# The last four weights of a transformer layer: loaded together into buffers of their own, and one part of a gate vector computed a step earlier

## Chip, cores, metric
One core of one Trainium2 chip runs the whole layer as one program. The metric is the time of an execution in device microseconds, as the median of several executions. Everything is fp32; the large matrix products run as pairs of rounded values (below).

## What is computed
The reference is one layer of a diffusion backbone over 512 latent tokens and 256 context tokens of width 1024: attention and gated linear attention side by side, merged and added to the stream, then a gated MLP with a 3x3 depthwise convolution. The change touches the end of the merge and the end of the MLP:

```python
mod = jax.nn.silu(c) @ w_ada[layer] + b_ada[layer]
sh1, sc1, gt1, sh2, sc2, gt2 = jnp.split(mod[:, None, :], 6, axis=-1)
...
out_lat = merge_branches(...)            # ends in  (...) @ w_out
x_lat = x_lat + gt1 * mix
h = modulate(rms_norm(x_lat, norm2_g[layer]), sh2, sc2)
val, gate = jnp.split(h @ w_up, 2, axis=-1)
gate = depthwise_conv_grid(gate, conv_w, conv_b, rows, cols)
x_lat = x_lat + gt2 * ((jax.nn.gelu(gate, approximate=False) * val) @ w_down)
return rms_norm(x_lat, final_g)
```

`gt2` is a vector of 1024 numbers, the last sixth of `mod`. `w_down` has 2816 rows, that is 22 blocks of 128 rows.

## The kernel before, in words
**Products.** A factor is held as a rounded high half and the rest, its low half. `split` (line 141) makes them from a loaded weight: ScalarE (ACT) casts the high half (`whi`), and GpSimd (POOL) or VectorE (DVE) subtracts to get the low half (`wlo`). `mm3` (line 146) then issues three matmuls: high by high, high by low, low by high. All instructions go through a helper, so almost every row of the profile has line 90 and is told apart by its tile names.

**The order of the work** is not written out: the framework's scheduler orders each engine's queue at build time, and tiles rotate through pools of fixed size. `tc.issue_after(x)` puts what a block issues behind the instruction x, on the engine that x runs on. Loads are issued by SyncE (SP) in a fixed order, and a load whose buffer is still in use holds up those behind it. PSUM has four single banks named `pb` and two double ones named `p`.

**Merge** (line 1378 on, eight steps j = 0 to 7): a projection for the gate, a projection of the second branch, sigmoid, and the merged block, split. Beside it the steps load the rows of `w_out` (`load_wo`, line 1356) and compute parts of `mod` on DVE. `gate_part(j)` (line 1098) computes a quarter of `gt2`: two loads of 512 KB from `w_ada` into tiles `wa` (two buffers) and eight DVE instructions `gt<-wa,csilu,gt`. Quarters 0 and 1 are done earlier, quarter 2 at merge step 6 and quarter 3 after the last four loads of `w_out`. Then `w_out_norm` (line 1432) multiplies by `w_out` per token tile, adds the residual, and normalises into `xn`, which TensorE (PE) transposes for the MLP; between its Square and its reciprocal root on ACT stand other casts as the scheduler puts them.

**MLP up** (line 1551): 22 column blocks, called columns here, i = 0 to 21. PE makes 24 matmuls for the gate and 24 for the value of a column into two `pb` banks; ACT starts the convolution (`ac<-pb`), DVE adds eight taps (`ac<-pb,cwT,ac`), ACT does gelu, DVE multiplies by the value bank (`ac<-pb,ac`), and the result is split. A column's banks are free for the column after next when its taps and its multiplication are done.

**MLP down.** Blocks 0 to 17 of `w_down` are taken as nine pairs by a 7-product scheme of Strassen's kind; sums of weights that it needs were written to DRAM before (`ws`). In the loop of line 1623, pair n loads two tiles of 512 KB, wa (half of it from `w_down`, half from `ws`) and wb (from `ws`), splits them, and PE does 24 matmuls: six each for p1, p6 (double banks), p7 and p5 (two `pb` banks each; p5 takes the banks of column 21). Staging tiles are `raw` (three buffers) and `rawd` (two), taken in turn by `raw_` (line 1574). `product` (line 1578) issues six matmuls. A second loop (line 1665) does the other three products.

Blocks 18 to 21, the last four weights, are used in plain form at the very end (`down`, line 1700). Before the change they are loaded by `load_down` (line 1586) within the pair loop, at pairs 1, 2, 4 and 5 (line 1636), each through the next staging tile; DVE scales the tile in place by `gt2`, and `split` makes the halves (`s`, in a pool of 30 tiles named `s4`). The tiles before the change are `rawd_7224`, `raw_7268`, `raw_7349` and `raw_7393`.

## Time and profile before

| | |
|---|---|
| executions shown | 895.63, 899.71, 902.21 us; median 899.71 |
| the profiled execution | 896.73 us, of which the span from the first to the last instruction is 894.9 |
| PE busy | 869.8 us, 97% of the span |
| DVE, ACT, POOL busy | 644.3, 412.7, 386.4 us |
| granted TensorE clock | 0.994 of full speed over the span |
| DMA | 130.53 MB, mean 146 GB/s |

The profile shows one execution. A timeline row gives start, duration, engine, operation, output and inputs, shape, count, and in brackets how long the engine sat idle before it and what ended the idle time. Rows of equal instructions that follow each other are merged with a count. The stages of interest are the end of the merge and the start of `w_out_norm` (about 455 to 512 us from the start of the span) and the change from MLP up to MLP down (about 745 to 830 us).

### The profile page before, as it was taken

Reading aid. Unit: us, or ns where it says so; the run is one execution under the profiler, and the core shown is the slowest. Engines: PE = TensorE matmul, PEld = TensorE weight load, DVE = VectorE, ACT = ScalarE, POOL = GpSimd, SP = SyncE. Lnnn points to the kernel's source line nnn. Section 1 sums busy time; section 2 is a strip of 40 time slices with the busy share of each in tenths; the row PEclk is TensorE's granted clock in tenths of the full one; section 3 lists DMA queues with packets and bytes.
Section 4 is the critical chain, followed back from the end, with each engine's and each line's share of the span. In section 5 each row is a group of like instructions: output and inputs, shape, how many; then the busy total and the mean of one; then the engine's idle time right before and its main releaser. Section 6 shows DMA issues by size and latency. Waiting matters only on the chain.

```text
span 894.9 us, 12819 instructions
## 1 busy us (share of the span) xinstructions
PE 869.8 (97%) x4794; PEld 738.8 (83%) x4794; DVE 644.3 (72%) x1049; ACT 412.7 (46%) x666; POOL 386.4 (43%) x258
## 2 busy tenths in 40 slices
PE   7999999999999999999999999999999998989996
PEld 5788899888888888888888799888888886768885
DVE  4477788876978686974775885966686665767866
ACT  4355676773463636344544333342343332456414
POOL 2512355450624343433743425776777765400004
PEclk9999999999999999999999999999999999999999
DMA  9970001216314141637973523455546555378602
GB/s 293 317 175 1 1 4 34 71 49 187 105 46 136 52 133 53 207 96 259 269 247 114 169 94 119 167 186 189 188 164 212 188 188 188 95 232 265 232 13 94
DMA packets 141648, 130.53 MB, mean 146 GB/s; under 512 B 7947, under 2 KB 122995, under 8 KB 141586
## 3 DMA queue, kind: packets, MB, share of 16 engines
q1 hardware_dynamic: 140354, 126.67, 46.5%
q10 hardware_dynamic: 832, 2.40, 0.7%
q8 instruction: 37, 0.61, 0.3%
q0 software_dynamic: 400, 0.65, 0.3%
q14 instruction: 25, 0.20, 0.1%
HBM read 115.87 MB, written 13.63 MB: 145 GB/s over the span
## 4 chain that ended last, share of the span: by engine, by line
PE 73%; DMA 9%; DVE 7%; ACT 4%; POOL 3%; issue 3%; SPq 0%; DVEq 0%; POOLq 0%; ACTq 0%
PE pb L90 36%; PE p L90 17%; PE pb L89 14%; PE p L89 6%; POOL wlo L90 2%; DMA raw<-in_w_ada_dram 2%; DVE s L90 2%; DMA raw<-in_w_down_dram 2%; DMA rawd<-in_w_down_dram 1%; DMA raw<-in_w_up_dram 1%; ACT s L90 1%; DMA ws<-rawd 1%; DVE ac L90 1%; DVE gt L90 1%; DMA xn<-in_w_ada_dram 1%
## 5 line engine op out<-in xcount | busy, mean ns | idle before, releaser
L90 POOL TENSOR_TENSOR wlo<-raw,whi 128x1024 fp32r<-128x1024 f32 (+1 forms) x91 | 210.6, 2323 | 224.4 <-ACT whi L90 193.7
L90 PE MATMUL pb<-s,whi 128*128 128x512 f32 (+1 forms) x906 | 272.4, 383 | 3.8 <-DVE ac L90 3.8
L90 PEld LDWEIGHTS pb<-s,whi 128*128 128x128 f32 x906 | 168.1, 189 | 36.6 <-issue 4.2
L90 PE MATMUL pb<-s,wlo 128*128 128x512 f32 (+1 forms) x453 | 173.4, 383 | 0.0
L90 ACT CAST whi<-raw 128x1024 fp32r<-128x1024 f32 (+1 forms) x106 | 102.9, 974 | 118.9 <-PE pb L90 46.4
L90 DVE SCALAR_TENSOR_TENSOR ac<-pb,cwT,ac 128x441 f32<-128x441 f32 (+2 forms) x160 | 110.9, 693 | 13.6 <-ACT ac L90 9.4
L89 PE MATMUL pb<-s,whi 128*128 128x512 f32 x320 | 101.2, 394 | 0.0
L90 PEld LDWEIGHTS pb<-s,wlo 128*128 128x128 f32 x453 | 85.5, 189 | 16.6
L90 PE MATMUL p<-s,s 128*128 128x512 f32 (+1 forms) x398 | 83.9, 364 | 0.6 <-DVE s L90 0.5
L90 PEld LDWEIGHTS p<-s,s 128*128 128x128 f32 x398 | 67.0, 189 | 12.8 <-DVE s L90 1.2
L89 PEld LDWEIGHTS pb<-s,whi 128*128 128x128 f32 x320 | 59.3, 188 | 11.5
L89 PE MATMUL pb<-s,wlo 128*128 128x512 f32 x160 | 62.8, 392 | 0.0
L90 PE MATMUL p<-whi,s 128*128 128x512 f32 x168 | 57.5, 400 | 0.0
L90 PE MATMUL pb<-whi,s 128*128 128x512 f32 x164 | 53.9, 391 | 1.9 <-DVE ac L90 1.2
L90 POOL TENSOR_TENSOR s<-s,edge 128x512 f32<-128x512 f32 x7 | 10.4, 1502 | 99.0 <-ACT s L90 99.0
L90 ACT ACTIVATE ac<-ac 128x512 f32<-128x512 f32 x22 | 13.9, 632 | 83.6 <-DVE ac L90 83.4
L90 PE MATMUL pb<-s,s 128*32 128x128 f32 (+2 forms) x340 | 46.2, 319 | 0.8 <-DMA s<-in_w_ada_dram 0.8
L90 DVE TENSOR_TENSOR pl<-pb,ph 128x512 fp32r<-128x512 f32 x48 | 33.0, 687 | 13.0 <-ACT ph L90 12.5
L90 PE MATMUL p<-kT,s 128*128 128x512 f32 (+1 forms) x192 | 41.2, 350 | 0.9 <-ACT P L90 0.9
L90 PEld LDWEIGHTS pb<-s,s 128*128 128x128 f32 (+1 forms) x340 | 36.1, 159 | 6.7 <-DVE rv L90 1.2
L90 PE MATMUL p<-s,whi 128*128 128x256 f32 (+1 forms) x156 | 38.6, 338 | 0.0
L90 PEld LDWEIGHTS pb<-whi,s 128*128 128x128 f32 x164 | 30.7, 188 | 9.0 <-DVE ac L90 1.6
(278 smaller groups left out, 1669.0 us busy)
## 6 DMA issues: line engine op xcount, KB each, us to landing
raw<-in_w_up_dram SPq DMA_DIRECT2D x44, 512.0 KB, 5.6
raw<-in_w_in_dram SPq DMA_DIRECT2D x28, 512.0 KB, 4.2
rawd<-in_w_down_dram SPq DMA_DIRECT2D x22, 512.0 KB, 5.6
s<-in_w_ada_dram SPq DMA_DIRECT2D x20, 512.0 KB, 6.8
ws<-rawd SPq DMA_DIRECT2D x18, 512.0 KB, 5.7
raw<-in_w_ada_dram SPq DMA_DIRECT2D x10, 512.0 KB, 7.6
xn<-in_w_ada_dram SPq DMA_DIRECT2D x10, 512.0 KB, 4.8
wa<-in_w_ada_dram SPq DMA_DIRECT2D x8, 512.0 KB, 5.8
```

The lines of the kernel that those rows point to most:

```text
L89: return fn(*args, **kw)
L90: ins = fn(*args, **kw)
```

## The change
It does two things. First, quarter 3 of `gt2` is computed at merge step 6 and quarter 2 at step 5, instead of after the loads of `w_out` and at step 6. Second, at pair 0 four tiles of the `s4` pool are taken and all four of the last weights are loaded into them, one load behind the other; the scaling and the split of weight n-1 are traced in pair n, n = 1 to 4, under `issue_after` of the last matmul of that pair's last product. They no longer use the staging tiles, so the pairs' own tiles fall on other buffers.

```diff
-            if j == 6:
+            if j in (5, 6):
                 with tc.issue_after(load[0].ins):
-                    gate_part(2, em_)
+                    gate_part(j - 3, em_)
         for k in range(4, 8):
             load_wo(k)
-        with tc.issue_after(load[0].ins):
-            gate_part(3, em_)
...
+        done = [None]
+
         def product(ps, hl, c, w, b, start, stop):
             for t in range(2):
...
-                mm3(ps[t], hl[0][:, cs], hl[1][:, cs], w[0][:, bs], w[1][:, bs], start, stop)
+                done[0] = mm3(ps[t], hl[0][:, cs], hl[1][:, cs], w[0][:, bs], w[1][:, bs], start, stop)
...
-        def load_down(k):
-
-            r = raw_()
-            SY.dma_start(out=r, in_=w_down[:, k, :])
-            tt(V, r, r, gt2, ALU.mult)
-            return r
...
-        wl_ = []
+        wl_, last = [], []
...
-            if n in (1, 2, 4, 5):
-                r = load_down(NF - NL + len(wl_))
-                wl_.append((S4([128, 1024]), S4([128, 1024])))
-                split(*wl_[-1], r, V)
+            if n == 0:
+                for k in range(NF - NL, NF):
+                    last.append(S4f())
+                    load[0] = SY.dma_start(out=last[-1], in_=w_down[:, k, :])
+            elif n < 5:
+                with tc.issue_after(done[0].ins):
+                    tt(V, last[n - 1], last[n - 1], gt2, ALU.mult)
+                    wl_.append((S4([128, 1024]), S4([128, 1024])))
+                    split(*wl_[-1], last[n - 1], V)
```

How the scheduler then orders the queues, at three places (numbers tell tiles apart; they differ between the two kernels where tiles are created in another order).

**DVE in columns 19 to 21 and the first pairs.** `ac_6961` is column 19, `gt_404` is gt2. First the piece of the difference in the taps of column 19:

```order
 L90 SCALAR_TENSOR_TENSOR ac_6961<-pb_6911,cwT_73,ac_6961 128x7x63
-L90 SCALAR_TENSOR_TENSOR ac_6961<-pb_6911,cwT_73,ac_6961 128x8x63
-L90 TENSOR_TENSOR rawd_7224<-rawd_7224,gt_404_2389 128x1024
-L90 SCALAR_TENSOR_TENSOR ac_6961<-pb_6911,cwT_73,ac_6961 128x8x63
+L90 SCALAR_TENSOR_TENSOR ac_6961<-pb_6911,cwT_73,ac_6961 128x8x63 x2
 L90 SCALAR_TENSOR_TENSOR ac_6961<-pb_6911,cwT_73,ac_6961 128x7x63
```

The scaling of the first of the last weights no longer stands in the middle of the eight taps of column 19. The second one (`raw_7268`) likewise leaves the taps of column 21. Next, before the change, the same queue at pairs 3 to 5 (`wlo_7285` is the low half of pair 3's wb, `wlo_7316` and `wlo_7322` those of pair 4, `wlo_7360` that of pair 5's wa):

```order
L90 TENSOR_TENSOR wlo_7285<-rawd_7282,whi_7284 128x1024
L90 TENSOR_TENSOR raw_7349<-raw_7349,gt_404_2389 128x1024
L90 TENSOR_TENSOR wlo_7316<-raw_7312,whi_7315 128x1024
L90 TENSOR_TENSOR s_1161_7353<-raw_7349,s_1160_7352 128x1024
L90 TENSOR_TENSOR wlo_7322<-raw_7319,whi_7321 128x1024
L90 TENSOR_TENSOR raw_7393<-raw_7393,gt_404_2389 128x1024
L90 TENSOR_TENSOR wlo_7360<-rawd_7356,whi_7359 128x1024
```

And of the change, the rows behind column 21 (`wlo_7241` and `wlo_7247` are the low halves of pair 2, `wlo_7283` and `wlo_7289` those of pair 3, `s_1115` is column 21's; `s_1129` to `s_1132` are the four last weights):

```order
L90 TENSOR_TENSOR wlo_7241<-rawd_7237,whi_7240 128x1024
L90 TENSOR_TENSOR s_1115_7137<-ac_7125,s_1115_7137 128x512
L90 TENSOR_TENSOR s_1129_7187<-s_1129_7187,gt_404_2389 128x1024
L90 TENSOR_TENSOR wlo_7247<-raw_7244,whi_7246 128x1024
L90 TENSOR_TENSOR s_1130_7189<-s_1130_7189,gt_404_2389 128x1024
L90 TENSOR_TENSOR s_1140_7234<-s_1129_7187,s_1139_7233 128x1024
L90 TENSOR_TENSOR s_1131_7191<-s_1131_7191,gt_404_2389 128x1024
L90 TENSOR_TENSOR wlo_7283<-raw_7279,whi_7282 128x1024
L90 TENSOR_TENSOR wlo_7289<-raw_7286,whi_7288 128x1024
L90 TENSOR_TENSOR s_1132_7193<-s_1132_7193,gt_404_2389 128x1024
```

Four scalings that stood in column 19, in column 21, at pair 4 and at pair 5 now all stand behind column 21, among the low halves of pairs 2 and 3.

**SP at the first pairs**, of the change (`raw_7286` is pair 3's wb, `rawd_7321` and `rawd_7328` are pair 4's two tiles):

```order
L90 DMA raw_7286<-ws_675_4129 128x1024
L90 DMA rawd_7321<-in_w_down_dram 128x512
L90 DMA rawd_7321<-ws_676_4130 128x512
L90 DMA s_1129_7187<-in_w_down_dram 128x1024
L90 DMA s_1130_7189<-in_w_down_dram 128x1024
L90 DMA s_1131_7191<-in_w_down_dram 128x1024
L90 DMA s_1132_7193<-in_w_down_dram 128x1024
L90 DMA rawd_7328<-ws_676_4130 128x1024
```

Before, the loads of the last weights stood one by one between those of the pairs. Now the four stand together behind the first tile of pair 4 and ahead of its second.

**SP at the end of the merge**, before (`wa` are the loads of the quarters of gt2):

```order
L90 DMA raw_4637<-in_w_br_gla_dram 128x4x128
L90 DMA wa_4671<-in_w_ada_dram 128x4x256
L90 DMA wa_4677<-in_w_ada_dram 128x4x256
L90 DMA raw_4742<-in_w_out_dram 128x1024
L90 DMA raw_4748<-in_w_out_dram 128x1024
L90 DMA raw_4754<-in_w_out_dram 128x1024
L90 DMA raw_4760<-in_w_out_dram 128x1024
L90 DMA wa_4766<-in_w_ada_dram 128x4x256
L90 DMA wa_4772<-in_w_ada_dram 128x4x256
L90 DMA raw_5106<-in_w_up_dram 128x8x128
```

and of the change:

```order
L90 DMA wa_4606<-in_w_ada_dram 128x4x256
L90 DMA wa_4612<-in_w_ada_dram 128x4x256
L90 DMA raw_4649<-in_w_br_gla_dram 128x4x128
L90 DMA raw_4754<-in_w_out_dram 128x1024
L90 DMA wa_4683<-in_w_ada_dram 128x4x256
L90 DMA raw_4760<-in_w_out_dram 128x1024
L90 DMA wa_4689<-in_w_ada_dram 128x4x256
L90 DMA raw_4766<-in_w_out_dram 128x1024
L90 DMA raw_4772<-in_w_out_dram 128x1024
L90 DMA raw_5106<-in_w_up_dram 128x8x128
```

The two loads of the last quarter no longer stand between the last load of `w_out` and the first of `w_up`; two loads of gt2 now stand ahead of the last step's `w_br_gla`, and two among the loads of `w_out`.

## The prediction
> **What bounds the kernel now.** I read the busy times first, then what PE waits for, then the stretches in which it waits, then the rows there.
>
> ```profile
> PE 869.8 (97%) x4794; PEld 738.8 (83%) x4794; DVE 644.3 (72%) x1049; ACT 412.7 (46%) x666; POOL 386.4 (43%) x258
> ...
> PE pb L90 <- DVE ac L90: 5.0, 2, 3.8
> ...
> PE p L90 <- DVE wlo L90: 2.1, 1, 2.1
> ...
> PE pb L90 <- DVE xn L90: 1.2, 1, 1.2
> ...
> PE pb L90 <- ACT whi L90: 0.7, 1, 0.7
> ```
>
> PE works for 97% of the span, so the matmuls bound it and a change can win only what PE waits, and what it is slowed. The waits for `ac`, `wlo` and `whi` fall into one stretch:
>
> ```profile
> 750.00:760.00 10.00, 6.58 (x30) 5.11 (x28) 4.47 (x7) 0.00 (x0) 2.09 (x1) 1.00 0.63 220
> 760.00:770.00 10.00, 9.60 (x35) 7.81 (x36) 8.04 (x11) 3.70 (x5) 5.20 (x2) 0.83 0.33 98
> ...
> 790.00:800.00 10.00, 9.28 (x41) 7.27 (x40) 6.43 (x6) 4.95 (x5) 0.00 (x0) 1.00 0.80 262
> 800.00:810.00 10.00, 7.91 (x28) 6.10 (x27) 7.19 (x7) 4.94 (x5) 0.00 (x0) 0.83 0.79 256
> ```
>
> Columns: busy us of PE, weight load, DVE, ACT, POOL, then granted clock, DMA share, GB/s. PE's rows there:
>
> ```profile
> 749.62 0.62 PE L90 MATMUL pb<-s,whi 128*128 128x512 f32 x2
> ...
> 756.20 0.39 PE L90 MATMUL pb<-s,wlo 128*128 128x512 f32 x1
> 760.40 0.82 PE L90 MATMUL pb<-s,whi 128*128 128x512 f32 x2 [3.82 <-DVE ac L90]
> ...
> 764.01 0.73 PE L90 MATMUL pb<-s,whi 128*128 128x512 f32 x2
> ...
> 780.70 0.39 PE L90 MATMUL pb<-wlo,s 128*128 128x512 f32 x1
> 782.28 0.50 PE L90 MATMUL pb<-whi,s 128*128 128x512 f32 x1 [1.20 <-DVE ac L90]
> ...
> 790.79 0.61 PE L90 MATMUL p<-whi,s 128*128 128x512 f32 x2
> 792.13 1.20 PE L90 MATMUL pb<-whi,s 128*128 128x512 f32 x4 [0.72 <-ACT whi L90]
> ...
> 802.74 0.39 PE L90 MATMUL p<-whi,s 128*128 128x512 f32 x1
> 805.23 0.79 PE L90 MATMUL p<-wlo,s 128*128 128x512 f32 x1 [2.10 <-DVE wlo L90]
> ...
> 808.38 0.74 PE L90 MATMUL p<-whi,s 128*128 128x512 f32 x2
> ```
>
> Between 749.62 and 756.20 start 29 matmuls, one each 0.227 us. From start to start, less that pace, the four waits cost 760.40-756.20-0.23 = 3.97, 782.28-780.70-0.23 = 1.35, 792.13-790.79-0.45 = 0.89 and 805.23-802.74-0.23 = 2.26, together 8.47 us. After the two long ones the clock is granted at 0.83 over 10 us: 9 matmuls take 3.61 us (760.40 to 764.01) and 7 take 3.15 (805.23 to 808.38), 1.57 and 1.56 us over the pace. So this stretch loses 8.47 + 3.13 = 11.6 us. What holds it is DVE:
>
> ```profile
> 743.25 7.03 DMA ws<-rawd
> 750.29 5.75 DMA rawd<-in_w_down_dram
> ...
> 747.96 2.89 DVE L90 SCALAR_TENSOR_TENSOR ac<-pb,cwT,ac 128x441 f32<-128x441 f32 x4 [0.94 <-ACT ac L90]
> 756.23 1.23 DVE L90 TENSOR_TENSOR rawd<-rawd,gt 128x1024 f32<-128x1024 f32 x1 [5.39 <-DMA rawd<-in_w_down_dram]
> 757.38 2.88 DVE L90 SCALAR_TENSOR_TENSOR ac<-pb,cwT,ac 128x504 f32<-128x504 f32 x4
> 761.01 0.69 DVE L90 TENSOR_TENSOR ac<-pb,ac 128x512 f32<-128x512 f32 x1 [0.76 <-ACT ac L90]
> ...
> 770.69 0.69 DVE L90 TENSOR_TENSOR ac<-pb,ac 128x512 f32<-128x512 f32 x1 [0.76 <-ACT ac L90]
> ...
> 779.69 1.23 DVE L90 TENSOR_TENSOR raw<-raw,gt 128x1024 f32<-128x1024 f32 x1 [1.61 <-DMA raw<-in_w_down_dram]
> 780.83 1.39 DVE L90 SCALAR_TENSOR_TENSOR ac<-pb,cwT,ac 128x448 f32<-128x448 f32 x2
> ...
> 784.91 0.69 DVE L90 TENSOR_TENSOR s<-ac,s 128x512 fp32r<-128x512 f32 x1 [0.96 <-ACT s L90]
> ...
> 794.93 1.23 DVE L90 TENSOR_TENSOR raw<-raw,gt 128x1024 f32<-128x1024 f32 x1 [1.60 <-DMA raw<-in_w_down_dram]
> 796.08 1.22 DVE L90 TENSOR_TENSOR wlo<-raw,whi 128x1024 fp32r<-128x1024 f32 x1
> ...
> 802.81 1.23 DVE L90 TENSOR_TENSOR raw<-raw,gt 128x1024 f32<-128x1024 f32 x1 [3.17 <-DMA raw<-in_w_down_dram]
> 803.95 1.22 DVE L90 TENSOR_TENSOR wlo<-rawd,whi 128x1024 fp32r<-128x1024 f32 x1
> ```
>
> Each of the four scalings (`gt`) stands at the head of DVE's queue and waits for its load, 11.8 us in all, with work of nearer need behind it: taps of columns 19 and 21, then low halves. The first load could not start before 750.29, when the write of `ws` had left its `rawd` tile.
>
> **The change, part by part.** It adds no work: four loads of 512 KB, four scalings, four casts, four subtractions and the eight-instruction quarters of gt2 are there before and after. What counts is where they stand and wait.
>
> *Column 19.* Without the scaling the four later taps follow the first four at once and end at 747.96 + 2.89 + 2.88 = 753.7. PE asks for the bank at 756.4, so 2.7 us are left. Gain 3.97 + 1.57 = 5.54. If the taps were late by all of that margin, the wait would begin again.
>
> *Column 21.* The multiplication of column 19 moves from 761.01 to 753.7 + 0.75 = 754.5. A column takes 770.69 - 761.01 = 9.68, so that of column 20 is at 764.2. From there to the last tap of column 21 it was 780.83 + 1.39 - 770.69 = 11.5, less the wait and the scaling (1.61 + 1.14): 8.8, thus 773.0. PE, no longer held, starts column 21 at 756.4 and ends it at 756.4 + 48 x 0.227 = 767.3; in the new order 31 matmuls of pairs 0 and 1 stand ahead of the first that writes a bank of column 21, so it asks at 774.4, with 1.4 us to spare. Gain 1.35.
>
> *Low halves of the pairs.* The four scalings now stand behind column 21. The first low half of pair 2 needs gelu, a table load and a cast on ACT first: before, it started at 784.91, 2.7 behind a last tap that ended at 782.2, and with 0.4 allowed for the casts it is about 776.1 now. In the new order the low half of pair 3's wa is the eighth row from there; at 1.14 us a row (794.93 to 796.08) and 0.6 for the half-size one it ends at 776.1 + 0.6 + 6 x 1.14 + 1.22 = 784.8. PE needs it after 17 + 24 + 6 matmuls from 774.4, at 785.1. That is no margin, 0.3 us. Do the loads come in time?
>
> ```profile
> 775.44 2.40 POOL L90 TENSOR_TENSOR wlo<-rawd,whi 128x1024 fp32r<-128x1024 f32 x1
> ...
> rawd<-in_w_down_dram SPq DMA_DIRECT2D x22, 512.0 KB, 5.6
> ```
>
> On SP they stand behind pair 4's first tile, which waits for POOL's fourth subtraction to leave its buffer. That ended at 777.84 and follows column 20, which is 6.5 us earlier: 771.3. The four are issued by 773.5, the first lands at about 772.2 + 5.6 = 777.8, just when DVE gets to it. Behind pair 4's tile, the third is the fourth of five (2.1 MB); at 262 GB/s that is 8.0 us and at most a landing near 781, wanted at 784.8 - 1.22 - 1.14 = 782.4. So the waits of 0.89 and 2.26 with 1.56 of clock, 4.7, should go, but a wait at pair 3 may come. From below it is nothing; from above it is one like that at 805.23, 2.26 + 1.56 = 3.8. With 0.3 us in hand I take 1.5.
>
> By the Trainium skill (TensorE: Matmul & The Clock Gate, Part 1), the clock halves only after an idle window of about 3.4 us. The 0.83 after 805.23 came behind 2.26 us, so the trace does not bear that out as a threshold. By the rule the clock part would be 1.57 alone, and the sum below 1.56 smaller.
>
> *The quarters of gt2.* One wait of PE stands at the end of the merge:
>
> ```profile
> 504.47 1.09 PE L90 MATMUL pb<-cst,xn 128*128 128x128 f32 x8 [1.21 <-DVE xn L90]
> ...
> 484.51 7.47 DMA raw<-in_w_up_dram
> ...
> 499.26 1.06 ACT L90 ACTIVATE xn<-x 128x1024 f32<-128x1024 f32 x1 [2.65 <-DVE x L90]
> ...
> 500.32 1.04 ACT L90 CAST whi<-raw 128x1024 fp32r<-128x1024 f32 x1
> ```
>
> The cast stands between the Square at 499.26 and the reciprocal root. In the new order it stands ahead of the Square, and its load is no longer behind two of gt2: the first load of `w_up` took 7.47 us there, near twice a lone one. So the cast is done before 499 and the root comes 1.04 sooner; the transposes wait 0.2 instead of 1.21. Gain 1.0; at most 1.21 + 0.16. If the cast's load is late, it holds the Square instead: 1.04 more, and with a clock loss of 1.6 that is -2.6. On SP, `wa_4683` waits until DVE has used up the first `wa`, with two `w_out` loads behind it; PE wants these behind 485, over 20 us later. On DVE the quarters stand among sums of the merge that had 1 to 2 us of idle time a step.
>
> **The sum:** 11.6 - 1.5 + 1.0 = 11.1 us. Against the profiled execution of 896.73 (span 894.9, 1.83 around it) that is 885.6, span 883.8. The median of the runs shown, 899.71, is 2.98 above that execution; I take the same difference from it: **888.6**.
>
> **Rivals.**
>
> *Does not do what it says.* The scalings are said to come only behind the pairs' matmuls, but the matmul is on PE and the block holds DVE and ACT instructions alone. In the order, the third scaling, of pair 3, stands ahead of a low half that pair 3's own matmuls read, so it cannot be behind them. I hold this for near certain (0.95); it changes no time, as the sum already goes by the order.
>
> *The loads bunch.* From 771.4 on, pair 3 needs 2.1 MB by 782.4 and pair 5's second tile, the eighth load, 4.2 MB by about 792. That asks for 190 to 210 GB/s against 220 to 262 in the three fuller stretches above. At 188 GB/s pair 3 is 1.6 late and pair 5 2.1, with one slowing 1.6: 5.3 instead of 1.5, gain 11.6 - 5.3 + 1.0 = 7.3, time 892.4. For it: four loads in a row with two tiles of pairs between and behind. Against it: the rates.
>
> *The waits only move.* DVE stays the bound from column 20 on, and the 1.4 and 0.3 us of margin are all negative by 2 us or more: only the first wait goes, gain 5.5 less a slower pair 3 of 3.8, time 898.0. Against it: DVE's 11.8 us of waiting goes.
>
> *Slower.* DVE stands at the third scaling while the five loads crawl. It decides below about 120 GB/s: there pair 3 is 6 us late and pair 5 another 3, each with a slowing, 12 us against 12.6 won. At 98 GB/s, the lowest row above, the third lands at 793 and pair 3 is 10 late, pair 5 then 8 more, with 3.2 of clock: 21, time 899.71 - 12.6 + 21 = 908. That row had only three loads to carry, so it speaks weakly.
>
> **Chances.** The forecast 0.62, the bunch 0.24, only moved 0.09, slower 0.05. The forecast's own range is a wait of 0 to 3.8 and an early gain of 0.5 to 1.4: 886.7 to 891.4. With the runs shown 6.6 us apart, 8 in 10 is 884.0 to 896.5. A change within 1% (9.0 us) is about what a measurement of this kernel cannot tell from none. The forecast reaches beyond it in most of its range, 0.57, the bunch hardly, 0.01: faster 0.58, within 1% 0.37, slower 0.05.
>
> **What would show it.** No row `rawd<-rawd,gt` among the taps; PE without a wait between column 20 and 21 and granted 1.00 at 760 to 770; four loads `s<-in_w_down` within 2 us behind 771, landing by 782.5; DVE's waits for `in_w_down` under 2 us in all; at most one PE wait for `wlo`, at pair 3; span near 884. Wrong: a wait over 1 us at the p5 banks (column chain), more than one wait for `wlo` or `whi` with DMA over 0.8 busy (bunch), or the transposes waiting longer than 1.21.

## The result, and the profile after

| | before | changed |
|---|---|---|
| median of 8 runs each | 897.77 us (895.25 to 902.21) | 889.65 us (886.93 to 892.55) |
| ratio, 95% interval | | 0.9905 [0.9879, 0.9932] |
| profiled execution, its span | 896.73, 894.9 us | 888.12, 885.9 us |
| granted clock over the span | 0.994 | 0.998 |

The change takes off 8.1 us by the medians and 9.0 by the two spans. The forecast was 11.1 off, to 888.6 us. The three runs that were shown with the kernel before had a median 1.9 higher than the eight do, so 888.6 is nearer to 889.65 than the forecast saving is to the measured one.

Of the changed kernel, the busy times of the page, and from the view of PE's waits those at the two places of the change:

```profile
PE 866.9 (98%) x4794; PEld 737.0 (83%) x4794; DVE 647.1 (73%) x1049; ACT 412.6 (47%) x666; POOL 383.8 (43%) x258
...
PE p L90 <- POOL s L90: 1.9, 1, 1.9
PE p L90 <- DVE xn L90: 1.8, 1, 1.8
...
PE p L90 <- DVE wlo L90: 0.6, 1, 0.6
```

The waits of 5.0 for `ac`, 2.1 for `wlo`, 1.2 for the transposes and 0.7 for `whi` are gone. In their place stand one of 0.6 for `wlo` and two that were not there, for `s` and for `xn`. The stretches of the changed kernel (busy us of PE, weight load, DVE, ACT, POOL, then granted clock, DMA share, GB/s) say where:

```profile
470.00:480.00 10.00, 8.22 (x39) 6.62 (x38) 8.16 (x11) 6.10 (x11) 2.49 (x1) 1.00 0.18 70
480.00:490.00 10.00, 8.13 (x36) 6.36 (x35) 5.91 (x8) 3.71 (x5) 5.70 (x2) 1.00 0.21 68
...
750.00:760.00 10.00, 10.00 (x46) 8.29 (x45) 6.95 (x10) 4.25 (x7) 5.11 (x3) 1.00 0.96 298
760.00:770.00 10.00, 10.00 (x46) 8.29 (x45) 7.09 (x11) 4.24 (x7) 5.20 (x3) 1.00 0.34 110
...
780.00:790.00 10.00, 9.43 (x42) 7.46 (x41) 9.56 (x10) 6.98 (x8) 0.00 (x0) 1.00 0.72 272
790.00:800.00 10.00, 10.00 (x46) 8.29 (x45) 10.00 (x10) 4.96 (x5) 0.00 (x0) 1.00 0.82 279
800.00:810.00 10.00, 10.00 (x46) 8.29 (x45) 7.26 (x8) 6.75 (x7) 0.00 (x0) 1.00 0.83 271
```

From 750 to 770 and from 790 on PE is busy throughout at clock 1.00, where before it had 6.58 us of ten, and 0.83 behind it. The lost work is now at 470 to 490, in the merge, where PE had no idle time before:

```profile
470.00:480.00 10.00, 10.00 (x48) 8.36 (x47) 5.99 (x10) 6.47 (x11) 1.96 (x2) 1.00 0.01 2
480.00:490.00 10.00, 10.00 (x46) 8.24 (x45) 4.88 (x5) 2.41 (x3) 5.29 (x2) 1.00 0.61 189
```

PE's rows there after the change, and the one wait left among the pairs:

```profile
477.23 0.50 PE L90 MATMUL p<-xn,one_r 128*128 128x512 f32 x1 [1.78 <-DVE xn L90]
485.79 4.42 PE L90 MATMUL p<-s,s 128*128 128x512 f32 x18 [1.87 <-POOL s L90]
...
788.02 0.50 PE L90 MATMUL p<-wlo,s 128*128 128x512 f32 x1 [0.57 <-DVE wlo L90]
```

To split the 9.0 us, set the start of each of PE's 4,794 matmuls against that of the same matmul before. Up to the 2,850th (end of the merge) the changed kernel is 0.57 us ahead. Through the end of the merge and the start of `w_out_norm` it falls to 2.31 behind, so the gate part **costs 2.88**. From pair 6 on it is 9.02 ahead, so the weights part **wins 11.33**.

DVE in columns 19 and 21, and the first scaling among the low halves of pairs 2 and 3:

```profile
750.71 5.81 DVE L90 SCALAR_TENSOR_TENSOR ac<-pb,cwT,ac 128x441 f32<-128x441 f32 x8 [0.93 <-ACT ac L90]
...
769.87 5.81 DVE L90 SCALAR_TENSOR_TENSOR ac<-pb,cwT,ac 128x441 f32<-128x441 f32 x8 [0.94 <-ACT ac L90]
...
781.07 1.23 DVE L90 TENSOR_TENSOR s<-s,gt 128x1024 f32<-128x1024 f32 x1 [0.44 <-DMA s<-in_w_down_dram]
```

The eight taps of a column are one row of 5.81 us; before, the scaling split them. The four scalings wait 0.44 us in all for loads, where they waited 11.8.

### The profile page after: what moved, and what is told of

It reads as the page before. It is cut to its first block, busy times and chain, and to the rows that moved or that the text cites. A ratio compares the mean times of both kernels' runs of the same rounds, so it can differ in the third digit from the quotient of the medians.

```text
span 885.9 us, 12813 instructions
## 1 busy us (share of the span) xinstructions
PE 866.9 (98%) x4794; PEld 737.0 (83%) x4794; DVE 647.1 (73%) x1049; ACT 412.6 (47%) x666; POOL 383.8 (43%) x258
## 4 chain that ended last, share of the span: by engine, by line
PE 81%; DMA 7%; issue 4%; DVE 4%; POOL 2%; ACT 2%; SPq 0%; POOLq 0%; DVEq 0%; ACTq 0%
PE pb L90 41%; PE p L90 20%; PE pb L89 14%; PE p L89 6%; DMA raw<-in_w_ada_dram 3%; DMA raw<-in_w_br_gla_dram 2%; POOL wlo L90 1%; POOL s L90 1%; DVE s L90 1%; DMA s<-in_w_down_dram 1%; DMA xn<-in_w_ada_dram 1%; ACT P L90 1%; DVE mx L90 1%; DVE kT L90 0%; DMA xn<-in_w_out_dram 0%
## 5 line engine op out<-in xcount | busy, mean ns | idle before, releaser
L90 ACT CAST ph<-pb 128x512 fp32r<-128x512 f32 x48 | 28.2, 587 | 20.7 <-PE pb L90 20.5
```

The costliest lines, as they stand in the source:

```text
L90: ins = fn(*args, **kw)
```

## Experiments

Twelve runs were made, of eleven kernels. Each expectation names its own theories. The theory held after the result was this: the weights part wins because the scalings no longer stand at the head of DVE's queue among the taps, and nothing else in it matters; the gate part loses because sixteen multiplications on DVE, in place of eight, now stand ahead of the last sums of the merge. The rivals: the loads gain by being early and together, or by relieving the staging tiles; the `issue_after` matters; the loss in the merge is one of late loads, or is only the difference between two executions.

In all timed kernels PE's matmuls stand in comparable order, so the table gives the time between the starts of three pairs of matmuls, worked out from the traces. 340 matmuls at the pace of 0.2267 us take 77.08.

| kernel | end of the merge (2,850 to 3,100) | columns (3,100 to 4,200) | column 18 into the pairs (4,200 to 4,540) |
|---|---|---|---|
| before | 54.57 | 218.06 | 89.26 |
| gate_only | 58.89 | 218.61 | 91.06 |
| after | 57.45 | 218.06 | 77.93 |
| noafter | 60.02 | 218.06 | 79.07 |
| gate_behind | 61.41 | 218.06 | 81.50 |
| weights_only | 55.11 | 218.06 | 80.39 |
| own_place | 57.81 | 218.06 | 81.42 |
| own_again | 55.01 | 218.06 | 77.07 |
| pool_scale | 55.88 | 218.06 | 81.15 |
| better | 56.35 | 218.06 | 78.64 |
| late | 53.17 | 223.84 | 81.52 |
| late_sums | 53.17 | 223.87 | 79.87 |
| late_spread | 53.17 | 225.12 | 82.23 |

Kernels of the same order at a place differ there by 1.1 to 4.4 us from one execution to the next (noafter and after; own_place and own_again), so a single cell settles only what is larger. The profiled execution of gate_behind was the longest of its six, 8.4 us above their median, and that of pool_scale the shortest, 4.5 below.

### The two parts apart: weights_only and gate_only

weights_only is the kernel before with the second, third and later pieces of the diff (from `done = [None]` on). gate_only has the first piece alone:

```diff
-            if j == 6:
+            if j in (5, 6):
                 with tc.issue_after(load[0].ins):
-                    gate_part(2, em_)
+                    gate_part(j - 3, em_)
         for k in range(4, 8):
             load_wo(k)
-        with tc.issue_after(load[0].ins):
-            gate_part(3, em_)
```

> The kernel before with the weights' part of the change alone; the quarters of gt2 stay where they were. Theory A (the alignment of the two traces: the weights' part wins 11.3 us, the gate's part costs 2.9): 897.8 - 11.3 = 886.5 us, between column 19 and the pairs only the wait of 0.6 us for wlo at pair 3, and the wait of 1.2 us for xn near 504 is still there. Theory B (my forecast: weights 10.1, gate 1.0): 887.7. Theory C (the gate's part changed nothing, and the whole gain of 8.1 in the medians is the weights'): 889.7.

> The kernel before with the quarters of gt2 one merge step sooner and nothing else. Theory A (the quarters delay the low half of the merged sum and with it two things behind it): PE waits 1.8 us for DVE's xn and 1.9 us for POOL's s near 477 and 486, no wait for the transposes near 504, together +2.9: 900.7 us. Theory B (my forecast): the transposes' wait goes and nothing takes its place, -1.0: 896.8 us.

weights_only took 890.88 us, ratio 0.9889 [0.9860, 0.9918]; gate_only 903.51, ratio 1.0026 [1.0003, 1.0050]. Of the 900.06 us before, that is by the ratios 10.0 won by the weights (7.4 to 12.6) and 2.3 lost by the quarters (0.3 to 4.5); by the medians it is 9.2 and 3.5. The two make 7.7 together (5.7 by the medians), and the whole change measured 8.1. The gate part alone shows the two new waits at the same matmuls as the change:

```profile
477.30 0.50 PE L90 MATMUL p<-xn,one_r 128*128 128x512 f32 x1 [1.64 <-DVE xn L90]
...
485.87 4.60 PE L90 MATMUL p<-s,s 128*128 128x512 f32 x12 [1.93 <-POOL s L90]
```

weights_only has no wait for `xn` there and one of 0.45 for `s`. These waits alone do not show that the quarters bring them: own_place, whose quarters are where they were, has 0.57 for `xn` and then

```profile
484.87 5.30 PE L90 MATMUL p<-s,s 128*128 128x512 f32 x15 [1.92 <-POOL s L90]
```

What does show it is the length of DVE's work in the merge, which the section on the prediction gives for the other runs too. weights_only has a wait of its own, which the changed kernel lacks in its profile:

```profile
752.24 0.70 PE L90 MATMUL pb<-s,whi 128*128 128x512 f32 x2 [1.42 <-DVE ac L90]
```

own_place shows below what makes it.

### Own buffers alone: own_place, own_again

The whole edit to the kernel before is one word. Loads, scalings and splits are traced at pairs 1, 2, 4 and 5, as before; only the tile comes from the `s4` pool:

```diff
         def load_down(k):
 
-            r = raw_()
+            r = S4f()
             SY.dma_start(out=r, in_=w_down[:, k, :])
```

> The kernel before with a buffer of its own for each of the last four weights, but loads, scalings and splits still traced one by one at pairs 1, 2, 4 and 5. In its order no scaling stands in the taps any more. Theory A (what counts is that no scaling waits at the head of DVE's queue with taps behind it; that the four loads go out together does not): as with the whole weights' part, -11.3: 886.5 us, no PE wait over 1 us from 745 to 830. Theory B (the four loads must be early): only the waits in columns 19 and 21 go, 3.97 + 1.57 + 1.35 = 6.9, and the waits at pairs 3 to 6 stay: 890.9 us.

> The kernel with own buffers and the loads at the pairs' places a second time, beside the last candidate on one chip. Theory A (it is as good as the loads together; what its first profile lost near 485 and 751 was late loads, not its order): ratio 0.986 to 0.990 again, the stretch from column 18 to the last pair without a wait of scaling, and another sum of waits in the merge and near 751 than 0.82 + 2.09 and 2.28. Theory B (those waits belong to its order): the same waits again.

own_place took 889.40 us, ratio 0.9871 [0.9844, 0.9899]; the same kernel again 889.46, ratio 0.9876 [0.9844, 0.9909]. So one word wins all that the weights part wins. The loads do not have to come together, nor early: in own_again they are issued at 775.4, 787.7, 792.4 and 799.7, where the first had been issued at 750.29. The first and the third of DVE's scalings in the second execution (own_again):

```profile
780.92 1.22 DVE L90 TENSOR_TENSOR s<-s,gt 128x1024 f32<-128x1024 f32 x1
...
794.12 1.22 DVE L90 TENSOR_TENSOR s<-s,gt 128x1024 f32<-128x1024 f32 x1 [2.74 <-DMA s<-in_w_down_dram]
```

With the other tile the scheduler puts the first scaling behind column 21. The third waits 2.74 us for its load, and PE waits for nothing between 745 and 830: at this place DVE has the lead to pay for it. Among the taps of column 19 it had 2.7 us, against 5.39 of wait and 1.14 of scaling.

The two executions differ in one more thing, an earlier instruction of the same kind, a sum of weights for `ws`, ahead of the taps of column 18. In own_place, DVE and then PE:

```profile
739.40 0.69 DVE L90 TENSOR_TENSOR rawd<-rawd 128x512 f32<-128x512 f32 x1 [5.47 <-DMA rawd<-in_w_down_dram]
```

```profile
750.78 0.70 PE L90 MATMUL pb<-s,whi 128*128 128x512 f32 x2 [2.12 <-DVE ac L90]
```

In own_again:

```profile
735.92 0.69 DVE L90 TENSOR_TENSOR rawd<-rawd 128x512 f32<-128x512 f32 x1 [3.69 <-DMA rawd<-in_w_down_dram]
```

The load of that sum took 8.48 us in own_place, 8.31 in weights_only, 6.20 in the profile of the change and 5.46 in pool_scale, at the same place of the program. At over 8 us PE waits 1.42 (weights_only) or 2.12, and behind the 2.12 it is slowed too; at about 6 it does not wait. The longest, 9.43 in gate_behind, goes with a wait of 2.54. So one load of 512 KB, queued for by DVE, goes with a good part of the 4 us between 77 and 81 in the table's last column. The change leaves this instruction where it was.

### The scaling on another queue: pool_scale

```diff
             r = raw_()
             SY.dma_start(out=r, in_=w_down[:, k, :])
-            tt(V, r, r, gt2, ALU.mult)
+            tt(G, r, r, gt2, ALU.mult)
```

> The kernel before with the four scalings on GpSimd instead of VectorE; staging tiles and the loads' places as before. Theory A (DVE's queue stood behind the loads): the taps of columns 19 and 21 no longer wait and PE's waits there go although the loads are as late as before; GpSimd takes 2.4 us a scaling and makes low halves of pairs 0 and 1 up to 1.6 late, with a slowing of the clock of 1.6 at most: 897.8 - 11.3 + 1.6 to 3.2 = 888.1 to 889.7 us. Theory B (the late loads hold PE, whoever scales): no gain, 897.8 us.

The staging tiles and the places of the loads are those of before; only the queue in which the scaling waits is GpSimd's. It took 894.42 us, ratio 0.9923 [0.9897, 0.9950], and the stage of the table fell from 89.26 to 81.15. GpSimd now does the waiting, and in this stretch PE waits for GpSimd once:

```profile
756.49 2.41 POOL L90 TENSOR_TENSOR rawd<-rawd,gt 128x1024 f32<-128x1024 f32 x1 [6.16 <-DMA rawd<-in_w_down_dram]
```

```profile
779.17 0.50 PE L90 MATMUL pb<-wlo,s 128*128 128x512 f32 x1 [1.62 <-POOL wlo L90]
```

A wait of 6.16 us for the same load costs nothing at column 19 when GpSimd stands in it, while PE's wait of 1.62 at pair 1 comes behind the next scaling, which GpSimd begins at 774.39 after 3.67 us more for its load. So the queue in which one waits cost most of the time, and neither the load nor the buffer by itself. By the ratios this run wins 6.9 us and own_place 11.6; the difference is about as large as their intervals allow for, and PE's wait of 1.62 and two more for low halves on DVE (0.76 and 0.64) are part of it.

### The directive: noafter

```diff
             elif n < 5:
-                with tc.issue_after(done[0].ins):
+                if True:
                     tt(V, last[n - 1], last[n - 1], gt2, ALU.mult)
```

> The changed kernel without the order to put scaling and split behind the pairs' matmuls. Theory A (that order names a matmul and holds no instruction of TensorE, so it does nothing): the same rows in the same order, so 889.7 us, and as a second profile of one order it shows what differs between executions: the waits for xn and for POOL's s again, 1.5 to 2.5 us each, if they belong to the order. Theory B (the order holds back the scalings): without it DVE meets loads that have not landed, 2 us or more slower.

The order of every engine is row for row that of the changed kernel. It took 892.10 us, ratio 0.9926 [0.9900, 0.9953], which overlaps with the change's 0.9905 [0.9879, 0.9932]. The directive does nothing, as the first rival of the prediction had it. The 2.4 us between two medians of the same order is a measure of how finely the other comparisons may be read.

### The merge: gate_behind, better

gate_behind is the changed kernel with the last quarter held behind the low half of step 6's merged sum on DVE:

```diff
-                sub(V, gl, gsum, f(gh))
+                low = V.tensor_tensor(out=gl, in0=gsum, in1=f(gh), op=ALU.subtract)
...
-            if j in (5, 6):
+            if j == 5:
                 with tc.issue_after(load[0].ins):
-                    gate_part(j - 3, em_)
+                    gate_part(2, em_)
+            elif j == 6:
+                with tc.issue_after(load[0].ins), tc.issue_after(low.ins):
+                    gate_part(3, em_)
```

> The changed kernel, with the eight multiplications of the last quarter of gt2 put behind the low half of the merged sum (xn) on VectorE; every load and every other engine's order stays. Theory A (the gate's part costs because these multiplications stand ahead of that low half): the waits for xn (2.03 from start to start) and for POOL's s behind it (2.04) go, and nothing comes for them: 889.7 - 4.1 = 885.6 us. Theory B (it costs because its loads come in a stretch where the DMA is busy): the waits stay, 889.7 us.

It took 888.71 us, ratio 0.9890 [0.9854, 0.9926], not to be told from the change. In its profiled execution the wait for `xn` falls to 0.83, and the one for `s` stays. DVE and PE:

```profile
465.19 1.10 DVE L90 SCALAR_TENSOR_TENSOR gt<-wa,csilu,gt 128x256 f32<-128x256 f32 x1 [1.34 <-DMA wa<-in_w_ada_dram]
```

```profile
488.79 1.65 PE L90 MATMUL p<-s,s 128*128 128x512 f32 x3 [1.94 <-POOL s L90]
```

DVE waited 1.34 us for the first quarter's load there. But the eight multiplications are not out of the way: they now stand between the low half `xn`, at 477.15, and the `sg` of step 7, at 483.28. That is 6.13 us, against 4.34 in the kernel before (472.10 to 476.44), and GpSimd's `s` comes late by it. So the run does not speak against the theory; it moves the same work behind the first of the two instructions that PE needs, and still ahead of the second.

better joins what the earlier runs pointed to: own_place, both quarters one step sooner with the last one held as above, a fifth `w_out` load ahead of the quarters, and the weights of column 1 behind the first reciprocal root:

```diff
-            r = raw_()
+            r = S4f()
...
+            if j == 7:
+                load_wo(4)
...
-        w0 = [up_weights(i) for i in range(2)]
+        w0 = [up_weights(0)]
+        with tc.issue_after(root0.ins):
+            w0.append(up_weights(1))
```

> Own buffers with the loads at the pairs' places, the quarters of gt2 as in the changed kernel but the last one's multiplications behind the merged sum's low half, the fifth weight of w_out split ahead of the last merge step's sigmoid, and two casts of w_up behind the first reciprocal root. Theory A (all that PE waits for in both stretches is work that stands in a queue behind what isn't needed yet): the weights' 11.3 and 1.7 to 3 us of the merge go, 897.8 - 13.0 to 14.3 = 883.5 to 884.8 us. Theory B (each of these moves makes a wait of its own elsewhere): no better than own buffers alone, 886.5 us.

It took 889.71 us, ratio 0.9895 [0.9870, 0.9920]; its profiled execution had the shortest span of all, 885.4. Against own_place (0.9871 and 0.9876) the three additions gave nothing that can be seen.

### The quarters out of the merge: late, late_sums, late_spread

late is own_place with quarters 2 and 3 moved into the columns: four loads at column 3, four multiplications each traced at columns 4, 6, 8 and 10.

```diff
+            if i == 3:
+                late = []
+                for j in (2, 3):
+                    for k0 in (0, 4):
+                        r = S4f()
+                        load[0] = SY.dma_start(out=k3(r, 4, 256), in_=w_ada[:, k0:k0 + 4, 5120 + j * 256:5376 + j * 256])
+                        late.append((j, k0, k3(r, 4, 256)))
+            if i in (4, 6, 8, 10):
+                j, k0, r3 = late.pop(0)
```

late_sums adds the order of column 1's weights from better, and gives two subtractions of the last sum of weights to GpSimd. Its load for that sum took 6.54 us, a length at which own_again (6.69) loses nothing either, so it does not test what that load costs. late_spread is late with each four held behind the value-bank multiplication of columns 7 to 10:

```diff
-            if i in (4, 6, 8, 10):
+            if i in (7, 8, 9, 10):
...
+                    with tc.issue_after(valued[0].ins):
+                        V.scalar_tensor_tensor(...)
```

> Own buffers with the loads at the pairs' places, and quarters 2 and 3 of gt2 taken out of the merge: their four loads go into buffers of their own in the columns of MLP up, and their multiplications, four at a time, are traced at columns 4, 6, 8 and 10. Theory A (in the merge VectorE's chain stands behind the quarters and their loads): the stretch of 250 matmuls from the last merge steps into w_out, 54.6 to 57.8 us in the profiles with the quarters as before and 57.5 to 61.4 with them sooner, is at most 54.9, without a wait for xn or for POOL's s; 1 to 3 us less than own buffers alone: 884 to 886 us. Theory B (VectorE has no room in the columns): waits of 1 us or more for taps between columns 4 and 11, 888 us or more.

> The kernel with the quarters in the columns, and two more moves: two casts of w_up stand behind the first reciprocal root, and the last of the sums of weights, whose first subtraction waits for a load at the head of VectorE's queue in column 17, is done on GpSimd. Theory A (whatever waits for a load at the head of VectorE's queue with taps behind it costs when the load is late): no wait for the transposes (1.4 less) and none for taps near 750, where four of nine profiles have one of 1.6 to 2.7: 881 to 884 us. Theory B (GpSimd is then late with low halves of columns 18 and 19): a wait for wlo there, no better than 885 us.

> As the kernel with the quarters in the columns, but each four multiplications are put behind the multiplication by the value bank of columns 7, 8, 9 and 10, so that they stand neither ahead of a load nor all in one column. Theory A (the wait of 4.1 with 1.7 of clock near 609 came from sixteen multiplications in one column): it goes, the merge keeps its short stretch of 53.2, and the time is 891.9 - 5.8 = 886 us, or 884 where no load of a sum of weights is late. Theory B (VectorE's columns have no room for 8 us more at all): waits of 1 us or more spread over columns 8 to 12, no better than 889 us.

late took 891.94 us, ratio 0.9916 [0.9887, 0.9945]; late_sums 892.40, ratio 0.9926 [0.9899, 0.9953]; late_spread 895.46, ratio 0.9945 [0.9921, 0.9969]. All three pass the end of the merge in 53.17 us, against a mean of 55.7 over the five kernels above that leave the quarters where they were (54.57 to 57.81) and of 58.8 over the three with both quarters sooner and nothing held (57.45 to 60.02). That the quarters cost PE time in the merge is thereby shown. But the columns, 218.06 before, now take 223.84 to 225.12. In late the scheduler put fourteen of the sixteen ahead of the last tap of one column, and PE waits there. Two rows of DVE, then one of GpSimd, then PE's:

```profile
595.49 2.54 DVE L90 SCALAR_TENSOR_TENSOR gt<-s,csilu,gt 128x256 f32<-128x256 f32 x1
...
598.55 0.87 DVE L90 SCALAR_TENSOR_TENSOR gt<-s,csilu,gt 128x256 f32<-128x256 f32 x2
```

```profile
595.36 2.39 POOL L90 TENSOR_TENSOR wlo<-raw,whi 128x1024 fp32r<-128x1024 f32 x1 [1.69 <-ACT whi L90]
```

```profile
609.22 0.89 PE L90 MATMUL pb<-s,whi 128*128 128x512 f32 x2 [3.92 <-DVE ac L90]
```

Two multiplications take 0.87 us at 598.55, with GpSimd idle. One alone takes 2.54 at 595.49, where GpSimd has begun 0.13 us before, and it ends just behind GpSimd's. Spread over four columns they cost 7.1 us, against 5.8 in late, in several smaller waits. late_spread, four of the multiplications on DVE, and PE's longest wait in the columns:

```profile
638.08 6.45 DVE L90 SCALAR_TENSOR_TENSOR gt<-s,csilu,gt 128x256 f32<-128x256 f32 x4
```

```profile
664.22 1.19 PE L90 MATMUL pb<-s,whi 128*128 128x512 f32 x2 [2.66 <-DVE ac L90]
```

Four multiplications took 6.45 us there, beside two of GpSimd's that follow each other. So the columns have no room for them. Moving the quarters there gives back more than the merge gains.

### How a late tap is paid: doses

weights_only with extra work on DVE ahead of the taps of five columns, `max(ac, ac)` into `ac`, which leaves its values as they are:

```diff
+    DOSE = {5: 6, 8: 7, 11: 8, 14: 9, 17: 10}
...
+            for _ in range(DOSE.get(i, 0)):
+                tt(V, ac, ac, ac, ALU.max)
```

> The kernel with the weights' part alone, and ahead of the taps of columns 5, 8, 11, 14 and 17 six, seven, eight, nine and ten maxima of the convolution tile with itself (128x512, 0.6 us each, the values stay as they are), to make PE wait a known time. With 2.7 us to spare in a column the waits should be near 1.0, 1.6, 2.2, 2.8 and 3.4 us. Theory A (the clock is granted lower for some 10 matmuls after any wait over about 2.1 us): 1.5 us more behind the last three and none behind the first two. Theory B (the rule of the Trainium skill, TensorE: Matmul & The Clock Gate, Part 1, an idle window of about 3.4 us): at most behind the last.

```profile
589.24 8.55 DVE L90 TENSOR_TENSOR ac<-ac 128x512 f32<-128x512 f32 x6 [0.87 <-ACT ac L90]
```

```profile
605.18 0.70 PE L90 MATMUL pb<-s,whi 128*128 128x512 f32 x2 [2.04 <-DVE ac L90]
...
728.88 1.19 PE L90 MATMUL pb<-s,whi 128*128 128x512 f32 x2 [9.40 <-DVE ac L90]
```

One execution: 921.53 us, span 919.6, clock 0.980. The doses came out larger than meant, since a maximum took 1.4 us here in the mean and not the 0.69 of other two-operand rows of 128x512. The five waits were 2.04, 7.54, 2.10, 9.40 and 5.54. Behind each, PE is slowed for some nine matmuls, behind the shortest as behind the longest. No wait came out short enough to show one without slowing.

## Why the prediction was right, and where it was not

The direction, the place and the mechanism hold, and 889.65 lies in the range. The sum was 3.0 too large by the medians and 2.1 by the spans, and that hides a larger error in one term: the quarters were put 3.9 too high, while the columns and pairs came 1.2 better than forecast and 0.57 was won ahead of the change. That 888.6 lies 1.05 from the measured median is luck beyond that, since the three runs shown lay 1.9 above the median of the eight. The ratio's interval, 0.9879 to 0.9932, has the line of 1% inside it, so the runs do not decide between "faster" (0.58) and "within 1%" (0.37).

**Column 19, column 21, the pairs (10.1 forecast: 11.6 less 1.5).** The profile gives 11.33; over four executions with this part (after, noafter, weights_only, gate_behind) the stage takes 79.7 in the mean against 90.2 of the two without, 10.4; the timing of the part alone says 10.0. The single steps, with 2.31 taken from the times after for what the merge lost:

| step | forecast | after |
|---|---|---|
| taps of column 19 end | 753.7 | 754.2 |
| multiplication of column 19 | 754.5 | 755.0 |
| multiplication of column 20 | 764.2 | 764.6 |
| last tap of column 21 | 773.0 | 773.4 |
| the four loads issued | by 773.5 | 772.6 to 774.6 |
| the first one lands | 777.8 | 778.7 |
| DVE's waits for `in_w_down` | under 2 | 0.44 |
| wait at pair 3 | 1.5 | 0.57 |

No wait between column 20 and 21, clock 1.00 where it was 0.83. The 1.5 for pair 3 was taken between 0 and 3.8; it was 0.57 (1.07 in weights_only, 1.05 in noafter), and no slowing behind it. What the sum did not have is the load of the sum of weights at column 18, which holds PE for 1.42 us in weights_only and, as the row shows, for more in gate_behind:

```profile
756.39 0.70 PE L90 MATMUL pb<-s,whi 128*128 128x512 f32 x2 [2.54 <-DVE ac L90]
```

These two are why the mean gain of 10.4 stays under 11.33.

**The quarters (+1.0 forecast, −2.9 in the profile, −2.3 timed).** The 1.21 us that the transposes waited are gone, but not by the way that was worked out. The cast did not come before 499; ACT waits for its load, and the Square stands behind it:

```profile
500.31 1.05 ACT L90 CAST whi<-raw 128x1024 fp32r<-128x1024 f32 x1 [2.50 <-DMA raw<-in_w_up_dram]
501.85 1.06 ACT L90 ACTIVATE xn<-x 128x1024 f32<-128x1024 f32 x1 [0.48 <-DVE x L90]
```

PE was itself late by then, so nothing hangs on it; own_place, where the quarters did not move and PE was late too, has no wait of the transposes either. The step that failed is the last sentence, "On DVE the quarters stand among sums of the merge that had 1 to 2 us of idle time a step". It was used as if that room were enough, and the multiplications were never added up against it. DVE in the merge before, quarter 2 with its eight multiplications:

```profile
460.50 5.32 DVE L90 SCALAR_TENSOR_TENSOR gt<-wa,csilu,gt 128x256 f32<-128x256 f32 x7 [0.64 <-DMA wa<-in_w_ada_dram]
...
466.34 0.47 DVE L90 SCALAR_TENSOR_TENSOR gt<-wa,csilu,gt 128x256 f32<-128x256 f32 x1
...
470.87 0.69 DVE L90 TENSOR_TENSOR sg<-pb,sg 128x512 f32<-128x512 f32 x1 [2.08 <-ACT sg L90]
472.10 1.23 DVE L90 TENSOR_TENSOR xn<-p,xn 128x1024 fp32r<-128x1024 f32 x1 [0.54 <-ACT xn L90]
```

And after, with the sixteen of two quarters, and below it GpSimd:

```profile
461.03 1.65 DVE L90 SCALAR_TENSOR_TENSOR gt<-wa,csilu,gt 128x256 f32<-128x256 f32 x1 [0.80 <-DMA wa<-in_w_ada_dram]
...
463.00 4.51 DVE L90 SCALAR_TENSOR_TENSOR gt<-wa,csilu,gt 128x256 f32<-128x256 f32 x7
...
468.33 0.48 DVE L90 SCALAR_TENSOR_TENSOR gt<-wa,csilu,gt 128x256 f32<-128x256 f32 x1 [0.23 <-DMA wa<-in_w_ada_dram]
...
469.34 1.00 DVE L90 SCALAR_TENSOR_TENSOR gt<-wa,csilu,gt 128x256 f32<-128x256 f32 x2
...
470.86 0.48 DVE L90 SCALAR_TENSOR_TENSOR gt<-wa,csilu,gt 128x256 f32<-128x256 f32 x1
471.53 3.91 DVE L90 SCALAR_TENSOR_TENSOR gt<-wa,csilu,gt 128x256 f32<-128x256 f32 x4 [0.19 <-DMA wa<-in_w_ada_dram]
475.36 0.68 DVE L90 TENSOR_TENSOR sg<-pb,sg 128x512 f32<-128x512 f32 x1
475.96 1.22 DVE L90 TENSOR_TENSOR xn<-p,xn 128x1024 fp32r<-128x1024 f32 x1
```

```profile
460.00 2.40 POOL L90 TENSOR_TENSOR wlo<-raw,whi 128x1024 fp32r<-128x1024 f32 x1 [2.68 <-ACT whi L90]
464.19 1.48 POOL L90 TENSOR_TENSOR wlo<-raw,whi 128x512 fp32r<-128x512 f32 x1 [1.78 <-ACT whi L90]
471.11 2.49 POOL L90 TENSOR_TENSOR s<-xn,s 128x1024 fp32r<-128x1024 f32 x1 [5.44 <-ACT s L90]
```

Eight took 5.32 + 0.47 = 5.79 us before; sixteen take 1.65 + 4.51 + 0.48 + 1.00 + 0.48 + 3.91 = 12.03. Of the 6.24 more, 8 x 0.48 = 3.84 is the work, and the other 2.40 is time in which a multiplication stands while GpSimd runs: each of the three stretched rows (1.65 for one, 4.51 for seven, 3.91 for four) lies beside one of GpSimd's. DVE had 2.08 + 0.54 us idle ahead of the two instructions that matter. So the `sg` of step 6 moves from 470.87 to 475.36 and the low half `xn` from 472.10 to 475.96; `xn` is the operand that PE waits 1.78 us for at 477.23, and GpSimd's `s` for the next block comes late in turn, at 485.79. That is the working which the step should have had, and the rows before gave its price: an estimate from them is 5.79 for eight more, less 2.08 + 0.54 of idle time, 3.2 us.

The same stretch in the other runs bears it out. It is taken from the start of the sum `s<-sg,s` ahead of the quarters (458.25 before, 459.15 after) to the start of `xn`, and to that of GpSimd's `s`; better has another order there.

| multiplications ahead of `xn` | runs | to `xn`, us | to GpSimd's `s`, us |
|---|---|---|---|
| none | late, late_sums, late_spread | 9.75 to 9.80 | 19.7 to 20.5 |
| eight | before, weights_only, own_place, own_again, pool_scale, doses | 13.85 to 14.20 | 21.29 to 21.64 |
| eight, and eight behind it | gate_behind | 14.39 | 23.62 |
| sixteen | after, noafter, gate_only | 16.81, 16.91, 17.99 | 24.23, 24.33, 25.42 |

The runs with the same count lie close together, whatever the execution, and each eight multiplications add some 3 to 4 us. So the cause of the longer stretch is the multiplications, and not a difference between executions.

The Trainium skill has a rule for it (SBUF — State Buffer, SBUF: two separate sides): DVE and GpSimd share a pair of ports under an exclusive lock, which a DVE instruction with two SBUF inputs needs while GpSimd reads SBUF, and the one that comes second stands still until the other has ended. The trace agrees. A multiplication of the quarters reads `wa` and `gt` and stands; the taps read one operand from a PSUM bank (`pb`), and the eight at 750.71 take 5.81, 0.73 each, no longer than anywhere else, though GpSimd runs beside them:

```profile
750.09 4.77 POOL L90 TENSOR_TENSOR wlo<-raw,whi 128x1024 fp32r<-128x1024 f32 x2 [2.10 <-ACT whi L90]
```

What **stays open** is how much PE's two waits owe to each of the parts, since a second thing makes them. When this stretch of DVE's begins, PE has begun 2,798 matmuls in the kernel before and in gate_only, 2,804 in the changed kernel, 2,810 in own_place and 2,815 in noafter. So DVE can be up to 17 matmuls, 3.9 us, later against PE from one execution to the next; what delays it was not followed. own_place has its two waits from that, with a stretch of the usual length; own_again, at 2,799, has none, and pool_scale, at 2,804, one of 0.99 for `s`. Late loads within the stretch add to it as well: 0.23 and 0.19 in the change's execution, 1.38 and 1.25 in gate_only.

**The rivals.** That the directive does nothing held. That the loads bunch did not: the four landed in time, with the DMA engines 0.72 to 0.83 busy from 780 to 810. That the waits only move, and the slower case, did not come. The term that went the wrong way was in none of them: they all looked at the pairs and none at the merge, where the price was put at +1.0 with a single lower end of −2.6 for another cause.

**The clock.** The prediction charged 1.6 us behind a wait of more than two. The merge's two waits of 2.0 (gaps of 2.26 and 2.27 from start to start) brought no slowing, gaps of 2.32 in own_place and gate_only did, and the last section has the rest. The Trainium skill (TensorE: Matmul & The Clock Gate, Part 1) puts the idle window at about 3.4 us; with gaps of 2.32 us enough, the runs here do not agree.

**Also open:** 2.2 to 5.2 us that some executions of the same order lose between 231 and 240 us from the start, far ahead of the change, and others do not. These were not followed.

**The best version** is own_place, at 0.987 and 0.988, one word from the kernel before. Its intervals overlap with the change's, so that it beats the change by the gate part's 2 us is likely by the parts, and not shown by their direct times.

## What to carry to other kernels

Where an in-order engine feeds the one that sets the time, look in its rows for an instruction that waits for a load ahead of work of nearer need; another buffer or another engine's queue can take that waiting away without the load coming any sooner. A wait counts only where the engine has no lead: DVE's 5.39 us at column 19 cost PE 3.97, its 2.74 at pair 4 (own_again) nothing. And when work is moved onto an engine "with idle time", add up what is moved against the idle time ahead of the next instruction that someone waits for, and price work on DVE that reads two SBUF operands by the rows that it has in that stretch, beside GpSimd (5.79 us for eight here, up to 2.54 for one), and not by a row alone (0.48).

## What the runs showed of the hardware

**The clock is granted lower behind gaps of about 2.3 us and more, and the price hardly depends on the gap.** From start to start of two full-size matmuls, with the trace's pace of 0.227 us:

| gap, start to start | what followed |
|---|---|
| up to 2.27 us, the change's 2.26 and 2.27 among them | no slowing; 0.18 us over the pace at most |
| 2.32 to 4.3 us | 1.6 to 1.8 us lost over seven to nine matmuls at 0.43 us, granted 0.83; 2.3 and 3.0 in two cases with other waits just ahead (noafter at 480.38, gate_behind at 488.79) |
| 5.9 to 9.8 us | about 1.9 to 2.3 us lost |

That holds in 19 of the 20 gaps of 2.32 us or more found in the runs. The exception is late_spread at 757.36, a gap of 3.02 us with clock 1.00 behind it; what differs there is not known. Nor does the slowing always begin at once: behind the 2.43 us at 605.18 in doses six matmuls come at the full pace first, behind the 2.48 at 805.23 in the kernel before none. So something besides the gap has a part in it, and the line at 2.3 us is where these few gaps divide, not a measured constant. In this kernel a gap pressed from 2.4 to 2.2 us would have been worth some 1.6 us more than its length.

**DVE's multiplications with two SBUF operands stand while GpSimd works,** as told above: the 128x256 multiplication takes 0.43 to 0.48 us alone and 2.54 when GpSimd has begun just before it, and two fifths of what the second quarter costs in the merge is such standing (2.40 of 6.24 us). The four scalings of the last weights read two SBUF operands too, and take 1.22 us each; GpSimd is idle from 780 to 810.

**The same load, issued at the same place, takes 5.5 to 9.4 us** from one execution to the next (pool_scale, gate_behind). A schedule that works at 6 and waits at 8 shows as noise of up to 4 us in the whole.
